# Mamba-2 stage: the convolutions of groups 2 to 5 begin one to three steps later, that of group 6 one step sooner

## Chip, cores and metric

One core of one Trainium2 chip runs the whole program. The metric is the time of one execution on the device in microseconds (us); of several executions the median is given. TensorE is written PE, VectorE DVE, ScalarE ACT, GpSimd POOL and SyncE SP, as in the profile.

## What is computed

A decoder trunk of two layers on 256 tokens of width 2048: attention with an MLP, then a Mamba-2 layer with an MLP, all in float32. The change lies in the Mamba-2 layer. Cut to what matters, it computes:

```python
zxbcdt = h @ w_in                                   # 2048 -> z 4096, x 4096, B 1024, C 1024, dt 64
xbc = silu(causal_depthwise_conv(xbc, conv_w, conv_b))     # 4 taps along the tokens
...
y_diag = einsum('blsgh,bsghp->blghp', cb[..., None] * decay, x_c)   # cb = C B^T per group, 8 groups of 8 heads
...
y = (y + d_skip * xs) * silu(z)
y = y * rsqrt(mean(y * y) + eps) * norm_g           # per group of 512 channels
return y @ w_out
```

The x channels fall into eight groups of 512. Each group needs its own convolution, its own 8 heads, its own gate with z and its own slice of the output projection.

## The kernel before

**Weights and PE.** All matmuls on weights are float32 made of three products: each weight tile is split into a rounded part `wh` (ACT, line 102) and the remainder `wl` (DVE, line 103). The unit of this work is a *half*: a tile of 128x1024 elements that holds 256 rows of a 512-wide weight block. The order listings number the halves: `wh557`, `wl557`. For each half `block` (line 328) issues 12 matmuls of 128x512 on PE: eight with `wh` (lines 339 and 340), then four with `wl` (line 343). Loads of raw halves run six ahead on SP's queue and conversions three ahead (`Flow`, line 72); there are four `wh` and four `wl` buffers, so a half can be converted once the half four places before it has been multiplied.

**Steps.** A block of 2048 rows has eight halves. After every two halves `block` calls `tick` (line 243). One such step runs whatever small pieces of work are due and then `pump` (line 1410), which handles up to two heads of the group in progress. A piece of work is placed by `self.later(n, fn)`: n steps after now. PE's order is the order in which the code issues. The instructions of DVE, ACT, POOL and SP are placed by the program's scheduler, so a piece need not stand exactly where its step was issued.

**The list.** In the second part of the Mamba-2 layer the order of blocks is the table `SSM_ORDER`: `B1` and `C1` are blocks of 8 halves for B and C, `z0` to `z7` the gate blocks, `o0a` to `o3` blocks of the output projection. A word `vg+n` is the convolution of group g. It has no matmul block of its own; it calls `x_conv(g, n)`, which places the pieces n steps after the block before it in the list:

```python
self.later(wait, lambda: fetch(whole, lambda: weight(3), lambda: load(2), lambda: weight(2), lambda: load(1)))
self.later(wait + 1, lambda: fetch(lambda: weight(1), lambda: load(0)))
self.later(wait + 3, mult)
self.later(wait + 4, some)
self.later(wait + 4, lambda: cb_group(g))
self.later(wait + 5, lambda: (total(), hq.extend((g, i) for i in range(8))))
self.later(wait + 6, tanh)
self.later(wait + 7, lambda: (silu(), ahead()))
```

**What one convolution issues.** On SP: the group's 128x1024 `xtm` tile and three shifted copies `tap` (512 KB each), and five weight rows `cw` (256 KB each). On DVE: line 1364 and three of line 1359 (tap times weight), four of line 1356 (adding them up), line 1384 (the end of silu), all of 128x1024; two of line 1311 (`cb`, 128x128) and line 1397 (`far`). On ACT: tanh (line 1380) and a part of `cb` (line 1316). On POOL: `ahead`'s product (line 1391). On PE: `cb` (lines 1307 and 1308), later `far` (line 1395). With `total` the group's heads enter the queue `hq`: per head four small ACT operations (lines 1431 and 1433), per four heads two DVE products (line 1438, `mt`). After the eighth head come `products` on PE (line 1451, 64 small matmuls), POOL's products (lines 1455 and 1457), `add` on DVE (line 1463), and two steps later `gate`: POOL (line 1491), ACT squares, DVE line 282, POOL's power (line 283), DVE lines 1495 and 1497, a DMA on POOL's queue (line 308), and three or four steps later transposes on PE, read out by lines 299 and 300. DVE also serves the z blocks (line 1479) and the output blocks (line 437).

Of the kernel before, what the change touches and what calls it, by code (L numbers as in the profile page):

```python
# [161 lines left out]
def part(key, src):  # L162

    def units(flow):
        ld = Load("raw", src)
        return [Unit(key, 2, 512, [ld], lambda: flow.halves(ld.tile, 1024))]
    return units
# [47 lines left out]
class Trunk:  # L215
# [959 lines left out]
    def ssm_body(self, sp, dp, gain, later):  # L1175
# [359 lines left out]

        for step in SSM_ORDER:
            kind, i = step[0], int(step[1])
# [11 lines left out]
            else:  # L1549
# [16 lines left out]
               [("x", 6, o) for o in range(3, 8)] + [("x", 7, o) for o in range(8)]]  # L1566
SSM_WEAVE = ("x x 0 x x 1 x x N40 2 x N41 x 3 x N42 M20 M21 x M22 M23 N43 x N30 N31 N32 N33",
             "x x 0 x x 1 x x N40 2 x x N41 3 x N42 M20 x M21 M22 x M23 N43 x N30 N31 N32 N33 x")
SSM_ORDER = ["v1+3", "B1", "C1", "v2+1", "z0", "z1", "v3", "z2", "z3", "v4", "o0a", "o0b", "v5", "z4", "z5", "v6", "o1a", "v7+1",
             "o1b", "z6", "z7", "o2a", "o2b", "o3"]  # L1570


def woven(p):
# [85 lines left out]
def sequence(d):  # L1659
# [45 lines left out]
    for p in range(2):  # L1705
        unit = seven(("s",), p, d["si"][:, 8:16])
        for tok in woven(p):
            if tok[0] == "s":
                seq.append(lambda flow, t=tok, unit=unit: [unit(flow, *t[2:])])
            else:  # L1710
                kind, i, o = tok
                seq.append(part(("si",) + tok, d["si"][o // 2, col(kind, i)][:, (o % 2) * 1024:(o % 2) * 1024 + 1024]))
    for step in SSM_ORDER:
        kind, i = step[0], int(step[1])
# [93 lines left out]
```

## Time and profile before

| | us |
|---|---|
| Median of 3 executions (2289.05 to 2290.42) | 2289.38 |
| The profiled execution, a separate one | 2292.69 |
| its span in the profile | 2290.9 |
| its PE busy | 2273.1 |
| its DVE busy | 1964.4 |
| its ACT busy | 1442.6 |
| its POOL busy | 284.9 |

The profile is of one execution; times in its views count from the start of the span. A row of a timeline gives start, duration, engine, line, operation, the tile written and the tiles read, how many instructions were merged, and in square brackets how long the engine was idle before it and what released it. The granted PE clock of this execution was 0.999 of full speed. The second part of the Mamba-2 layer, which `SSM_ORDER` sets, lies between about 1170 and 1610 us.

### The profile page before, as it was taken

Reading aid. Unit: us, or ns where it says so; the run is one execution under the profiler, and the core shown is the slowest. Engines: PE = TensorE matmul, PEld = TensorE weight load, DVE = VectorE, ACT = ScalarE, POOL = GpSimd, SP = SyncE. Lnnn points to the kernel's source line nnn. Section 1 sums busy time; section 2 is a strip of 40 time slices with the busy share of each in tenths; the row PEclk is TensorE's granted clock in tenths of the full one; section 3 lists DMA queues with packets and bytes.
Section 4 is the critical chain, followed back from the end, with each engine's and each line's share of the span. In section 5 each row is a group of like instructions: output and inputs, shape, how many; then the busy total and the mean of one; then the engine's idle time right before and its main releaser. Section 6 shows DMA issues by size and latency. Waiting matters only on the chain.

```text
span 2290.9 us, 30854 instructions
## 1 busy us (share of the span) xinstructions
PE 2273.1 (99%) x10881; PEld 1881.4 (82%) x10881; DVE 1964.4 (86%) x2257; ACT 1442.6 (63%) x2044; POOL 284.9 (12%) x339
## 2 busy tenths in 40 slices
PE   9999999999999999999999999999999999999999
PEld 7898888888888888887788788888888887888887
DVE  7786698999899897888889998976989988989985
ACT  7775476566566666566577676564666665666663
POOL 1440000000000000100002532230000000000000
PEclk9999999999999999999999999999999999999999
DMA  8545678888888877758798888866788887798874
GB/s 315 172 152 163 210 234 264 261 253 263 269 253 261 268 231 246 244 180 281 234 359 288 290 289 303 307 215 218 211 261 252 256 275 234 253 277 243 266 232 163
DMA packets 176026, 569.74 MB, mean 249 GB/s; under 512 B 20192, under 2 KB 29344, under 8 KB 175872
## 3 DMA queue, kind: packets, MB, share of 16 engines
q1 hardware_dynamic: 147808, 498.24, 64.9%
q0 software_dynamic: 16320, 56.88, 11.8%
q10 hardware_dynamic: 11744, 12.66, 1.7%
q8 instruction: 85, 1.39, 0.2%
q14 instruction: 69, 0.57, 0.1%
HBM read 542.23 MB, written 6.41 MB: 239 GB/s over the span
## 4 chain that ended last, share of the span: by engine, by line
PE 87%; DVE 6%; DMA 4%; issue 2%; ACT 1%; POOL 0%; SPq 0%; ACTq 0%; DVEq 0%
PE acc L339 10%; PE acc L340 10%; PE acc L343 10%; PE yp L618 9%; PE yp L619 8%; PE yp L617 8%; PE st L618 7%; PE st L619 7%; PE st L617 7%; DVE wl L103 3%; DMA wraw<-mi 2%; DMA wraw<-si 1%; ACT wh L102 1%; PE st L1162 1%; PE st L1160 1%
## 5 line engine op out<-in xcount | busy, mean ns | idle before, releaser
L102 ACT ACTIVATE wh<-wraw 128x1024 fp32r<-128x1024 f32 (+1 forms) x818 | 857.5, 1053 | 528.5 <-PE acc L340 176.7
L103 DVE TENSOR_TENSOR wl<-wraw,wh 128x1024 fp32r<-128x1024 f32 (+1 forms) x818 | 989.2, 1227 | 180.5 <-ACT wh L102 169.7
L617 PE MATMUL yp<-wh,k 128*128 128x512 f32 x896 | 349.7, 390 | 0.0
L618 PE MATMUL yp<-wl,k 128*128 128x512 f32 x896 | 349.1, 390 | 0.1
L619 PE MATMUL yp<-wh,k 128*128 128x512 f32 x896 | 349.0, 390 | 0.0
L102 ACT ACTIVATE wh<-wrx 128x1024 fp32r<-128x1024 f32 x192 | 203.2, 1059 | 174.8 <-PE yp L619 98.4
L103 DVE TENSOR_TENSOR wl<-wrx,wh 128x1024 fp32r<-128x1024 f32 x192 | 233.0, 1219 | 37.1 <-ACT wh L102 36.2
L618 PEld LDWEIGHTS yp<-wl,k 128*128 128x128 f32 x896 | 168.5, 188 | 35.5 <-DVE wl L103 0.5
L619 PEld LDWEIGHTS yp<-wh,k 128*128 128x128 f32 x896 | 168.5, 188 | 35.2
L339 PE MATMUL acc<-wh,k 128*128 128x512 f32 x496 | 196.9, 397 | 0.3 <-ACT k L299 0.3
L617 PEld LDWEIGHTS yp<-wh,k 128*128 128x128 f32 x896 | 168.5, 188 | 34.9
L340 PE MATMUL acc<-wh,k 128*128 128x512 f32 x496 | 193.7, 391 | 0.6 <-DVE k L300 0.6
L339 PE MATMUL acc<-wh,xt 128*128 128x512 f32 x480 | 191.8, 400 | 0.6 <-ACT wh L102 0.6
L340 PE MATMUL acc<-wh,xt 128*128 128x512 f32 x480 | 187.7, 391 | 0.0
L617 PE MATMUL st<-wh,xt 128*128 128x512 f32 x448 | 177.7, 397 | 0.0
L619 PE MATMUL st<-wh,xt 128*128 128x512 f32 x448 | 174.9, 390 | 0.0
L618 PE MATMUL st<-wl,xt 128*128 128x512 f32 x448 | 174.7, 390 | 0.0
L199 POOL DMA_DIRECT2D wrx<-mi x56 | 49.1, 877 | 726.1 <-DVE wl L103 515.5
L617 PE MATMUL st<-wh,sN 128*128 128x512 f32 x336 | 133.4, 397 | 0.8 <-ACT wh L102 0.8
L618 PE MATMUL st<-wl,sN 128*128 128x512 f32 x336 | 131.8, 392 | 2.1 <-DVE wl L103 2.0
L343 PE MATMUL acc<-wl,k 128*128 128x512 f32 x496 | 132.7, 389 | 0.0
L619 PE MATMUL st<-wh,sN 128*128 128x512 f32 x336 | 131.4, 391 | 0.0
(342 smaller groups left out, 3806.6 us busy)
## 6 DMA issues: line engine op xcount, KB each, us to landing
wraw<-mi SPq DMA_DIRECT2D x256, 512.0 KB, 5.7
wraw<-mo SPq DMA_DIRECT2D x256, 512.0 KB, 5.2
wraw<-si SPq DMA_DIRECT2D x160, 512.0 KB, 5.7
wraw<-so SPq DMA_DIRECT2D x64, 512.0 KB, 5.1
wrx<-mi SPq DMA_DIRECT2D x56, 512.0 KB, 5.2
wrx<-mi POOLq DMA_DIRECT2D x56, 512.0 KB, 7.7
wraw<-wo SPq DMA_DIRECT2D x32, 512.0 KB, 4.1
tap<-xD SPq DMA_DIRECT2D x24, 512.0 KB, 8.3
```

Source lines behind the costliest of these rows:

```text
L102: self.last = nc.scalar.activation(h[:, v], raw[:, v], AF.Copy)
L103: self.last_lo = nc.vector.tensor_tensor(lo[:, v], raw[:, v], h[:, v].bitcast(F32), ALU.subtract)
L199: nc.gpsimd.dma_start(st["b11"].tile, quarter(d, 1, 0), accum_op=ALU.add)
L339: nc.tensor.matmul(accs[t][:, :n], ah, wh[:, q, :], start=first and kt + q == 0, stop=False)
L340: nc.tensor.matmul(accs[t][:, :n], al, wh[:, q, :], start=False, stop=False)
L343: nc.tensor.matmul(accs[t][:, :n], lhs(kt + q, t)[0], wl[:, q, :], start=False, stop=en and q == nk - 1)
L617: nc.tensor.matmul(b, ah, wh, start=first and q == 0, stop=False)
L618: nc.tensor.matmul(b, ah, wl, start=False, stop=False)
L619: nc.tensor.matmul(b, al, wh, start=False, stop=last and q == 1)
L1160: nc.tensor.matmul(bank[onto], ah, wh, start=done + q == 0 and not skip, stop=False, skip_group_check=skip)
L1162: nc.tensor.matmul(bank[onto], ah, wl, start=False, stop=done == 3 and q == 1, skip_group_check=skip)
```

## The change

One table is written anew; no function changes.

```diff
-SSM_ORDER = ["v1+3", "B1", "C1", "v2+1", "z0", "z1", "v3", "z2", "z3", "v4", "o0a", "o0b", "v5", "z4", "z5", "v6", "o1a", "v7+1",
-             "o1b", "z6", "z7", "o2a", "o2b", "o3"]
+SSM_ORDER = ["v1+3", "B1", "C1", "v2+2", "z0", "z1", "v3+1", "z2", "z3", "v4+3", "o0a", "o0b", "v5+1", "z4", "v6+3", "z5", "o1a",
+             "v7+1", "o1b", "z6", "z7", "o2a", "o2b", "o3"]
```

Convolutions 2, 3 and 5 begin one step later and 4 three steps later. Convolution 6 stood behind `z5` and now stands behind `z4` with three steps to wait; a z block has four steps, so it begins one step sooner. From one convolution's start to the next's there were 6, 7, 8, 8, 8, 5 steps (1 to 2, 2 to 3, and so on to 7), and there are now 7, 7, 10, 6, 6, 6. The sequence of weight halves is the same, and so are the counts of rows on PE (10011), SP (999) and POOL (336); ACT and DVE differ only in how like rows are merged.

DVE between the halves 554 and 556, in blocks `z0` and `z1`. Before:

```order
L103 TENSOR_TENSOR wl554_11473<-wraw554_11372,wh554_11472 128x1024
L1230 SCALAR_TENSOR_TENSOR s2_824_11413<-s2_825_11414,cst_96,s2_824_11413 128x253
L1364 TENSOR_TENSOR xtm2_11300<-xtm2_11300,cw2_3_11302 128x1024
L1359 TENSOR_TENSOR tap2_2_11304<-tap2_2_11304,cw2_2_11306 128x1024
L1233 SCALAR_TENSOR_TENSOR k4_813_11155<-s2_826_11424,s2_824_11413 128x512
L1479 SCALAR_TENSOR_TENSOR s2_828_11442<-s2_828_11442,acc_816_11160 128x512
L1479 SCALAR_TENSOR_TENSOR s2_829_11445<-s2_829_11445,acc_817_11161 128x512
L1356 TENSOR_TENSOR xtm2_11300<-xtm2_11300,tap2_2_11304 128x1024
L103 TENSOR_TENSOR wl555_11527<-wraw555_11390,wh555_11526 128x1024
L282 TENSOR_SCALAR st_837_11503<-st_827_11441 128x2
L103 TENSOR_TENSOR wl556_11545<-wraw556_11452,wh556_11544 128x1024
```

and now:

```order
L103 TENSOR_TENSOR wl554_11473<-wraw554_11368,wh554_11472 128x1024
L1230 SCALAR_TENSOR_TENSOR s2_824_11409<-s2_825_11410,cst_96,s2_824_11409 128x253
L1438 TENSOR_TENSOR mt12_11508<-mt12_11508,cb1_11133 128x512 x2
L103 TENSOR_TENSOR wl555_11520<-wraw555_11386,wh555_11519 128x1024
L1233 SCALAR_TENSOR_TENSOR k4_813_11155<-s2_826_11420,s2_824_11409 128x512
L1479 SCALAR_TENSOR_TENSOR s2_828_11442<-s2_828_11442,acc_816_11160 128x512
L1479 SCALAR_TENSOR_TENSOR s2_829_11445<-s2_829_11445,acc_817_11161 128x512
L103 TENSOR_TENSOR wl556_11538<-wraw556_11452,wh556_11537 128x1024
```

The three pieces of group 2's convolution (`xtm2`, `tap2_2`) have left, and the score products of group 1 (`mt12`) have moved up.

DVE between the halves 556 and 557, just behind. Before:

```order
L103 TENSOR_TENSOR wl556_11545<-wraw556_11452,wh556_11544 128x1024
L1495 TENSOR_TENSOR st_839_11507<-st_838_11504,rs0_150 128x2
L1359 TENSOR_TENSOR tap2_1_11308<-tap2_1_11308,cw2_1_11353 128x1024
L1497 SCALAR_TENSOR_TENSOR s2_828_11442<-xtm0_10549,st_839_11507,gb_834_11495 128x512
L1497 SCALAR_TENSOR_TENSOR s2_829_11445<-xtm0_10549,st_839_11507,gb_834_11495 128x512
L1356 TENSOR_TENSOR xtm2_11300<-xtm2_11300,tap2_1_11308 128x1024
L1311 SCALAR_TENSOR_TENSOR cb2_11565<-sm_842_11562,tri_8827 128x128 x2
L1397 TENSOR_TENSOR far1_11570<-sm_843_11568,edge_8831 128x512
L1438 TENSOR_TENSOR mt12_11515<-mt12_11515,cb1_11133 128x512 x2
L103 TENSOR_TENSOR wl557_11587<-wraw557_11470,wh557_11586 128x1024
```

and now:

```order
L103 TENSOR_TENSOR wl556_11538<-wraw556_11452,wh556_11537 128x1024
L1364 TENSOR_TENSOR xtm2_11343<-xtm2_11343,cw2_3_11345 128x1024
L282 TENSOR_SCALAR st_837_11496<-st_827_11441 128x2
L1359 TENSOR_TENSOR tap2_2_11347<-tap2_2_11347,cw2_2_11349 128x1024
L1495 TENSOR_TENSOR st_839_11500<-st_838_11497,rs0_150 128x2
L1397 TENSOR_TENSOR far1_11562<-sm_842_11560,edge_8831 128x512
L1497 SCALAR_TENSOR_TENSOR s2_828_11442<-xtm0_10549,st_839_11500,gb_834_11488 128x512
L1497 SCALAR_TENSOR_TENSOR s2_829_11445<-xtm0_10549,st_839_11500,gb_834_11488 128x512
L1356 TENSOR_TENSOR xtm2_11343<-xtm2_11343,tap2_2_11347 128x1024
L103 TENSOR_TENSOR wl557_11579<-wraw557_11470,wh557_11578 128x1024
```

Between `wl554` and `wl557` there stood five 128x1024 pieces of group 2 and its two `cb` pieces; three 128x1024 pieces stand there now, and the other two and the `cb` pieces follow behind `wl558`.

DVE between the halves 616 and 617, in block `o1b`, where the convolution of group 6 runs. Before:

```order
L103 TENSOR_TENSOR wl616_13393<-wraw616_13320,wh616_13392 128x1024
L1364 TENSOR_TENSOR xtm6_13243<-xtm6_13243,cw6_3_13245 128x1024
L1359 TENSOR_TENSOR tap6_2_13247<-tap6_2_13247,cw6_2_13249 128x1024
L437 TENSOR_TENSOR x01_143<-acc_941_13318,x01_143 128x512
L1356 TENSOR_TENSOR xtm6_13243<-xtm6_13243,tap6_2_13247 128x1024
L437 TENSOR_TENSOR x11_147<-acc_942_13319,x11_147 128x512
L103 TENSOR_TENSOR wl617_13422<-wraw617_13338,wh617_13421 128x1024
```

and now:

```order
L103 TENSOR_TENSOR wl616_13364<-wraw616_13291,wh616_13363 128x1024
L1359 TENSOR_TENSOR tap6_1_13125<-tap6_1_13125,cw6_1_13218 128x1024
L1311 SCALAR_TENSOR_TENSOR cb6_13384<-sm_935_13381,tri_8827 128x128
L1356 TENSOR_TENSOR xtm6_13117<-xtm6_13117,tap6_1_13125 128x1024
L1311 SCALAR_TENSOR_TENSOR cb6_13384<-sm_935_13381,tri_8827 128x128
L1397 TENSOR_TENSOR far5_13389<-sm_936_13387,edge_8831 128x512
L1497 SCALAR_TENSOR_TENSOR s2_915_12902<-xtm4_12422,st_942_13403,gb_937_13391 128x512
L1438 TENSOR_TENSOR mt44_13334<-mt44_13334,cb5_13002 128x512 x2
L437 TENSOR_TENSOR x01_143<-acc_933_13289,x01_143 128x512
L437 TENSOR_TENSOR x11_147<-acc_934_13290,x11_147 128x512
L103 TENSOR_TENSOR wl617_13430<-wraw617_13309,wh617_13429 128x1024
```

The second tap of group 6, its `cb`, the `far` part and the score products of group 5 and a gate product of group 4 now stand together in front of one half.

## The prediction

> **What bounds the kernel now.** First the page: its head, the busy times and the chain of work that ended last.
>
> ```profile
> span 2290.9 us, 30854 instructions
> ...
> PE 2273.1 (99%) x10881; PEld 1881.4 (82%) x10881; DVE 1964.4 (86%) x2257; ACT 1442.6 (63%) x2044; POOL 284.9 (12%) x339
> ...
> PE 87%; DVE 6%; DMA 4%; issue 2%; ACT 1%; POOL 0%; SPq 0%; ACTq 0%; DVEq 0%
> ```
>
> PE is busy for 2273.1 of 2290.9 us, so all its pauses together are 17.8 us. The change adds no PE instruction and removes none. It can only win or lose PE's pauses, and only those in the stretch it touches. Those are shown by PE's waits between 1170 and 1580 us (total, times, longest):
>
> ```profile
> engine line waited for: us in total, times, longest us
> PE acc L343 <- DVE wl L103: 2.6, 1, 2.6
> PE acc L340 <- DVE k L300: 0.6, 1, 0.6
> PE acc L339 <- ACT k L299: 0.3, 1, 0.3
> ```
>
> There are three, 3.5 us together, and one of them is 2.6 us. The timeline of PE shows where it stands:
>
> ```profile
> 1262.75 1.07 PE L343 MATMUL acc<-wl,xt 128*128 128x512 f32 x4
> ...
> 1265.25 0.39 PE L340 MATMUL acc<-wh,xt 128*128 128x512 f32 x1
> 1268.22 1.19 PE L343 MATMUL acc<-wl,xt 128*128 128x512 f32 x4 [2.58 <-DVE wl L103]
> 1269.34 2.09 PE L1451 MATMUL y<-xtm,mt 128*64 128x64 f32 x64
> ```
>
> The last `wh` matmul of a half starts at 1265.25, and the four `wl` matmuls come only at 1268.22, after 2.58 us of idling. The 64 small matmuls of group 1 behind them name the half: it is 557, the last of `z0`'s. Why its `wl` was late is in DVE's timeline.
>
> ```profile
> 1250.63 0.48 DVE L1230 SCALAR_TENSOR_TENSOR s<-s,cst,s 128x253 f32<-128x253 f32 x1
> 1251.02 1.22 DVE L1364 TENSOR_TENSOR xtm<-xtm,cw 128x1024 f32<-128x1024 f32 x1
> 1252.16 1.22 DVE L1359 TENSOR_TENSOR tap<-tap,cw 128x1024 f32<-128x1024 f32 x1
> 1253.29 0.69 DVE L1233 SCALAR_TENSOR_TENSOR k<-s,s 128x512 f32<-128x512 f32 x1
> 1253.89 1.28 DVE L1479 SCALAR_TENSOR_TENSOR s<-s,acc 128x512 f32<-128x512 f32 x2
> 1255.09 1.92 DVE L1356 TENSOR_TENSOR xtm<-xtm,tap 128x1024 f32<-128x1024 f32 x1
> 1256.93 2.31 DVE L103 TENSOR_TENSOR wl<-wraw,wh 128x1024 fp32r<-128x1024 f32 x1
> 1259.17 0.15 DVE L282 TENSOR_SCALAR st<-st 128x2 f32<-128x2 f32 x1
> 1259.24 1.21 DVE L103 TENSOR_TENSOR wl<-wraw,wh 128x1024 fp32r<-128x1024 f32 x1
> 1261.06 0.16 DVE L1495 TENSOR_TENSOR st<-st,rs 128x2 f32<-128x2 f32 x1 [0.62 <-POOL st L283]
> 1261.14 1.23 DVE L1359 TENSOR_TENSOR tap<-tap,cw 128x1024 f32<-128x1024 f32 x1
> 1262.29 1.41 DVE L1497 SCALAR_TENSOR_TENSOR s<-xtm,st,gb 128x512 f32<-128x512 f32 x2
> 1263.61 1.22 DVE L1356 TENSOR_TENSOR xtm<-xtm,tap 128x1024 f32<-128x1024 f32 x1
> 1264.75 0.48 DVE L1311 SCALAR_TENSOR_TENSOR cb<-sm,tri 128x128 f32<-128x128 f32 x2
> 1265.15 0.68 DVE L1397 TENSOR_TENSOR far<-sm,edge 128x512 f32<-128x512 f32 x1
> 1265.74 1.28 DVE L1438 TENSOR_TENSOR mt<-mt,cb 128x512 f32<-128x512 f32 x2
> 1266.94 2.35 DVE L103 TENSOR_TENSOR wl<-wraw,wh 128x1024 fp32r<-128x1024 f32 x2
> ```
>
> The last row holds `wl557` and `wl558`; the first of them ends near 1268.1. No bracket stands at that row, so the copy `wh557` was there and DVE simply came late. Between 1250.6 and 1268.1 it paused once, for 0.62 us. This is a queue on a full engine.
>
> **The change, part by part.** *The late half.* By the two orders, DVE's work between `wl554` and `wl557` loses one L1359, one L1356 and two L1311 (front, first two places). From start to start these took 1.15 (1261.14 to 1262.29), 1.14 (1263.61 to 1264.75) and 0.40 (1264.75 to 1265.15): 2.69 us. The score products of group 1 move up but are counted in both. So `wl557` ends near 1268.1 - 2.7 = 1265.4, and PE wants it 2.58 before 1268.22, at 1265.64. The wait goes, with 0.2 us to spare. A second gain stands beside it: an L1359 now lies between L282 and L1495 and covers the 0.62 us pause for POOL's power. I take the gain at 2.6 us. Its bounds are 1.7 (one more row slowed as at 1256.93, 2.31 us instead of 1.22, less the 0.2 to spare) and 2.6, for a wait cannot give more than itself.
>
> *What is late next.* With PE 2.6 us earlier every later half is wanted 2.6 us earlier, while DVE, which has no free time there, does the same work: by wl561 both orders have done the same. The next thin place is half 565, here its `wl` on DVE and its matmuls on PE:
>
> ```profile
> 1287.30 2.32 DVE L103 TENSOR_TENSOR wl<-wraw,wh 128x1024 fp32r<-128x1024 f32 x1
> ...
> 1293.13 1.07 PE L343 MATMUL acc<-wl,xt 128*128 128x512 f32 x4
> ```
>
> It was ready 1293.13 - 1289.62 = 3.5 us ahead. After the change that is 3.5 - 2.6 = 0.9, plus 0.6 for one L1438 that now stands behind it: 1.5 us. That holds, so I cost it at nothing; one slowed row (1.1 us) fits, two do not.
>
> *Groups 4 to 6, six steps apart instead of eight.* The convolution work taken out of the earlier part lands here. Adding the orders' rows from `wl589` to `wl637` (1.14 us per 128x1024 row, 0.60 per 128x512, and 0.40, 0.20 and 0.67 for L1230, L1311 and L1497, all start to start as above), DVE has 117.9 us of work before and 129.8 after. The window between those two halves shows how full it was (us, DVE busy):
>
> ```profile
> 1363.80:1501.00 137.20, 127.16 (x139) 1.00 0.85 294
> ```
>
> 127.2 busy of 137.2. So 117.9 of table work cost 9.3 us more than the table, and 10.0 us were free; 11.9 more nearly fill it. What decides is the lead, how long a half is ready before PE wants it. Where DVE waits for buffers alone the lead is full:
>
> ```profile
> 1386.78 1.22 DVE L103 TENSOR_TENSOR wl<-wraw,wh 128x1024 fp32r<-128x1024 f32 x1 [1.24 <-ACT wh L102]
> ...
> 1395.85 1.07 PE L343 MATMUL acc<-wl,xt 128*128 128x512 f32 x4
> ```
>
> That is half 599: 1395.85 - 1388.00 = 7.8 us. PE's own pace is in three more of its rows, the matmuls with `wl` of halves 566, 567 and 568:
>
> ```profile
> 1296.75 1.07 PE L343 MATMUL acc<-wl,xt 128*128 128x512 f32 x4
> 1299.47 1.07 PE L343 MATMUL acc<-wl,xt 128*128 128x512 f32 x4
> 1302.87 1.07 PE L343 MATMUL acc<-wl,xt 128*128 128x512 f32 x4
> ```
>
> A half alone takes 2.72 us (1296.75 to 1299.47), `cb`'s matmuls behind half 567 add 0.68 (3.40 to the next), `far`'s behind 565 add 0.90 (1293.13 to 1296.75 is 3.62). In the new order DVE's rows outrun PE at three places. Between halves 588 and 593 it has 16.6 us against 14.3 (five halves and a `cb`), between 613 and 617 15.2 against 12.5 (four, `cb`, `far`; the third place in the front), between 624 and 629 18.7 against 15.2 (five, `cb`, `far`). The lead falls by 2.3, 2.7 and 3.5, to 5.5, 5.1 and 4.3. The extra 9.3 us are four groups' to the window, 2.3 each, and leave 3.2, 2.8 and 2.0. So these three cost nothing either; from below nothing is to be won, since PE did not wait here, and from above the bound is the slower rival below.
>
> *What else moves, at nothing.* SP's loads of a convolution move with it, ahead of other weight loads than before; ACT's longest wait for weights shows what that can do:
>
> ```profile
> ACT wh L102 <- DMA wraw<-si: 14.1, 10, 3.3
> ```
>
> 3.3 us at most, ten times, and none reached PE; a full lead of 7.8 covers it. If the lead is down to 4.3 it still does. ACT (63% busy) and POOL keep their instructions. PE's small blocks stand behind other halves; each takes its time wherever it stands, and I allow 0.3 us either way for neighbours. The waits of 0.6 and 0.3 us are those of group 7's transposes, which keep their place.
>
> *The sum.* 2292.69 - 2.6 = 2290.1 for an execution like the profiled one (span 2288.3). The profiled one was 3.3 us above the median of 2289.38, so the median goes to 2289.38 - 2.6 + 0.1 = **2286.9**. A measurement of this kernel can tell about 0.2%, 4.6 us, from no change; the forecast is a gain of 0.11%.
>
> **What POOL does to this sum.** Two of its rows and one where DVE stood still:
>
> ```profile
> 1254.65 3.51 POOL L1491 TENSOR_TENSOR xtm<-s,xtm 128x512 f32<-128x512 f32 x2 [12.08 <-DVE s L1479]
> ...
> 1271.46 10.41 POOL L1455 TENSOR_TENSOR xtm<-xtm,gb 128x512 f32<-128x512 f32 x2 [6.13 <-issue]
> ...
> 1501.87 2.54 POOL L1455 TENSOR_TENSOR xtm<-xtm,gb 128x512 f32<-128x512 f32 x2 [3.08 <-issue]
> ```
>
> A pair of POOL products takes 2.54 us alone and 10.41 beside a DVE that never pauses; and DVE rows beside L1491 took 1.92 and 2.31 instead of 1.22. Either may pay. The Trainium skill, SBUF — State Buffer, "Who interferes with whom", says that a VectorE instruction with two SBUF inputs contends with a GpSimd one that reads SBUF, and that whoever issues first keeps the shared ports for its whole instruction while the other stands. By that rule, with POOL always first, DVE is charged the whole of each POOL instruction and the sum is the slower rival's 2296.5; with DVE always first it is the forecast's. The rows above agree that one side stands, and here it is mostly POOL.
>
> **Rivals.** *The wait moves* (0.20). PE, no longer held at 557, is held at 565 or at one of the three crowded places, because two rows are slowed there. For it: 565's lead is only 1.5 us. Against it: everywhere else 2 us and more are left. Price: two slowed rows, 2.2 us, or one with the 0.8 us that L1495 can wait (L282 and L1495 now stand together ahead of `wl566`), against 1.5: about 0.7 each time, twice 1.3. Time 2288.2.
>
> *Nothing happens* (0.07). The late half stays late: the loss of 2.7 us of rows is made up by other slow rows, as POOL's L1491 falls on L1364 and `wl556` now. Against it: L1491 starts when L1479 ends, and the rows ahead of L1479 last as long in both orders (two of 1.14 before, one of 1.14 and two of 0.60 now). Time 2289.4.
>
> *Slower* (0.09). Between halves 588 and 629 DVE is nearly full, and it pays for POOL. Six POOL products per group at 1.27 us are 7.6, with the pause of 0.6 before L1495 8.2 us per group. Against leads of 5.5, 5.1 and 4.3 this makes waits of 2.7, 3.1 and 3.9, 9.7 in all; less 2.6 the kernel is 7.1 us slower, 2296.5. It turns against the change from about 5.8 us per group on, where the three waits sum to 2.5. Against it stands the 2.3 per group measured in that window.
>
> **How the numbers follow.** The forecast has 0.64. Its own range is 2285.9 (the other two waits shrink as well) to 2288.0. The range 2285.9 to 2289.6 takes in the forecast, the moved wait and the unchanged case; the slower rival is left out. For over 0.2% faster 4.6 us would be needed, and this stretch has 3.5 us of waits: 0.02. For over 0.2% slower, half of the slower rival: 0.05. Within 0.2%: 0.93.
>
> **What would show it.** Right: no PE wait for `wl` at half 557 between 1170 and 1580 us; DVE ending `wl557` before L340 of that half is done; the same 2.0 us of small matmuls behind it; DVE's busy share between halves 589 and 637 near 139 of 138 us of PE time, that is with hardly a pause, and no PE wait there; about 1.5 us of lead at 565. Wrong: a wait of PE for `wl` at 565, 593, 617 or 629; DVE rows of over 2 us in numbers; PE's spacing of 2.72 us per half changed.

## The result, and the profile after

The changed kernel takes 2298.73 us (median of 6 runs, 2294.64 to 2303.03) against 2289.9 us for the one before (6 runs, 2288.6 to 2292.85): 1.0039 times as long, interval 1.0029 to 1.0049. That is 8.8 us or 0.39% slower, where 0.11% faster was forecast; it lies outside the range given. The profiled execution took 2298.48 us.

The page of the kernel after: its head, the busy times and the chain that ended last.

```profile
span 2296.7 us, 30847 instructions
...
PE 2277.0 (99%) x10881; PEld 1882.1 (82%) x10881; DVE 1970.8 (86%) x2257; ACT 1442.1 (63%) x2044; POOL 280.0 (12%) x339
...
PE 91%; DVE 3%; DMA 3%; ACT 1%; issue 1%; POOL 1%; SPq 0%; DVEq 0%; ACTq 0%; POOLq 0%
```

PE has the same 10881 instructions, but is busy for 3.9 us longer (2273.1 before). So besides the pauses something made its instructions themselves slower. PE's waits of the kernel after, between 1170 and 1580 us (total, times, longest):

```profile
PE sm L1395 <- DVE k L300: 4.6, 1, 4.6
PE acc L339 <- ACT k L299: 1.3, 1, 1.3
PE acc L343 <- DVE wl L103: 1.1, 1, 1.1
PE acc L340 <- DVE k L300: 0.3, 1, 0.3
```

There were three waits of 3.5 us in all; there are four of 7.3. Where they stand is in PE's timeline of the kernel after. The first and last rows are marks: the transposes behind half 549, the products behind 557, and the products behind half 641, between which PE has the same work in both kernels.

```profile
1243.31 0.60 PE L1220 MATMUL sm<-ident,s 128*128 128x128 f32 x4
...
1267.62 2.09 PE L1451 MATMUL y<-xtm,mt 128*64 128x64 f32 x64
...
1281.42 1.21 PE L343 MATMUL acc<-wl,xt 128*128 128x512 f32 x4 [1.10 <-DVE wl L103]
...
1327.32 0.50 PE L339 MATMUL acc<-wh,k 128*128 128x512 f32 x1 [1.27 <-ACT k L299]
1328.13 0.50 PE L340 MATMUL acc<-wh,k 128*128 128x512 f32 x1 [0.30 <-DVE k L300]
...
1405.12 0.59 PE L1307 MATMUL sm<-k,k 128*128 128x256 f32 x2
...
1405.69 0.53 PE L322 MATMUL sm<-ident,tr 128*128 128x128 f32 x4
1410.84 1.63 PE L1395 MATMUL sm<-s,cb 128*128 128x512 f32 x2 [4.62 <-DVE k L300]
1411.48 1.41 PE L339 MATMUL acc<-wh,xt 128*128 128x512 f32 x1
1412.69 0.63 PE L340 MATMUL acc<-wh,xt 128*128 128x512 f32 x1
1413.12 0.63 PE L339 MATMUL acc<-wh,xt 128*128 128x512 f32 x1
...
1534.97 2.08 PE L1451 MATMUL y<-xtm,mt 128*64 128x64 f32 x64
```

The same marks in the kernel before (that of 557 stands in the prediction, at 1269.34):

```profile
1242.63 0.60 PE L1220 MATMUL sm<-ident,s 128*128 128x128 f32 x4
...
1524.66 2.09 PE L1451 MATMUL y<-xtm,mt 128*64 128x64 f32 x64
```

From 549 to 557 PE took 26.71 us before and 24.31 after: 2.40 us are won, nearly what was forecast, and of the wait at 557 a stop of 0.12 us is left. From 557 to 641 it took 255.32 before and 267.35 after: 12.03 us are lost, so between these marks the kernel is 9.6 us slower. The medians differ by 8.8 us and the two profiled executions as a whole by 5.8 (spans 2290.9 and 2296.7): behind half 641 the one before took 4.5 us more, 1.7 of it by a stretch of halved clock at 1908.55. In the 12.03 are

- 1.10 us at half 561, the wait for `wl`;
- 1.57 us at half 576, the first that multiplies group 1's transposed gate output (lines 299 and 300);
- 4.62 us behind half 601, where `far` of group 4 (line 1395) waits;
- slow matmuls behind the last two. At 1412.69 and 1413.12 they follow each other in 0.43 us and not in 0.23.

The windows of the kernel after, behind those two waits (us, busy PE, PEld, DVE, ACT, POOL, then the granted PE clock):

```profile
1329.60:1333.00 3.40, 3.40 (x10) 2.64 (x9) 3.40 (x5) 3.24 (x9) 0.72 (x1) 0.54 0.46 153
1411.40:1414.80 3.40, 3.40 (x9) 2.34 (x8) 1.12 (x2) 0.00 (x0) 0.00 (x0) 0.52 0.69 194
```

For 3.41 us each the clock is halved, and half of that time is lost: 1.7 us each, 3.4 together. With the waits, 7.29 by their brackets, that makes 10.7. The other 1.3 us lie mostly at the same places and in a stop of 0.12 us at 1294.0, since a wait costs more than its bracket: at half 561 the last `wh` row starts at 1279.93 and the `wl` row at 1281.42, 1.49 us apart where 0.23 is usual, which is 1.26 us for a bracket of 1.10.

Why `far` waited is in DVE's timeline of the kernel after:

```profile
1407.22 1.22 DVE L1359 TENSOR_TENSOR tap<-tap,cw 128x1024 f32<-128x1024 f32 x1
1408.47 1.22 DVE L1356 TENSOR_TENSOR xtm<-xtm,tap 128x1024 f32<-128x1024 f32 x1
1409.62 0.48 DVE L1311 SCALAR_TENSOR_TENSOR cb<-sm,tri 128x128 f32<-128x128 f32 x2
1410.02 0.68 DVE L300 TENSOR_TENSOR k<-sm,k 128x512 fp32r<-128x512 f32 x1
1410.61 1.21 DVE L103 TENSOR_TENSOR wl<-wraw,wh 128x1024 fp32r<-128x1024 f32 x1
```

`far`, `cb` and these transposes all write into the pool `sm`, which has two banks (line 229: `self.sm = pool("sm", 2, space=PSUM)`). A bank here is a tile in PSUM, the memory that PE writes its results to; the program gives it to the next block only when the readers of the last one are done. Behind half 601 the new order issues three of them in one step: `cb` of group 5, a transpose of group 3, `far` of group 4. The bank of `cb` is kept until ACT has read it, one step later (`far_part`). `far` needs the other one, and that holds the transposes, which PE had written by 1406.2. DVE reads them in line 300 behind two long rows of convolution 5 and the `cb` rows, from 1410.02 to 1410.70; at 1410.84 PE goes on. In the order before, `far` of group 4 stood behind half 611 with nothing else of `sm` there, and it did not wait:

```profile
1432.99 1.02 PE L1395 MATMUL sm<-s,cb 128*128 128x512 f32 x2
```

### The profile page after: what moved, and what is told of

Read it like the earlier page. It is cut to its first block, busy times and chain, and to the rows that moved or that the text cites. A ratio compares the mean times of both kernels' runs of the same rounds, so it can differ in the third digit from the quotient of the medians.

```text
span 2296.7 us, 30847 instructions
## 1 busy us (share of the span) xinstructions
PE 2277.0 (99%) x10881; PEld 1882.1 (82%) x10881; DVE 1970.8 (86%) x2257; ACT 1442.1 (63%) x2044; POOL 280.0 (12%) x339
## 4 chain that ended last, share of the span: by engine, by line
PE 91%; DVE 3%; DMA 3%; ACT 1%; issue 1%; POOL 1%; SPq 0%; DVEq 0%; ACTq 0%; POOLq 0%
PE acc L339 10%; PE acc L340 10%; PE acc L343 9%; PE yp L619 9%; PE yp L617 9%; PE yp L618 9%; PE st L618 7%; PE st L619 7%; PE st L617 7%; DVE wl L103 2%; DMA wraw<-si 1%; PE st L1162 1%; PE yp L339 1%; PE yp L340 1%; PE sm L324 1%
```

## The experiments

All kernels are changed from the one after. The order tables are given by the words that differ. "Stretch" is the time from PE's products behind 557 to those behind 641, as above: 255.32 us before, 267.35 after. The kernel before was timed again beside each group of runs, with medians of 2289.82 to 2290.40 us; distances from it are from the median beside the run. Each experiment was profiled in one execution.

**A bank of another pool for one block**

```diff
-                    b = self.bank(False)
+                    b = self.yp.tile([P, 512], F32, tag="yp", name=self.name("yp")) if g == 4 else self.bank(False)
```

> The changed order; only the far product of group 4 (line 1395) is written to a bank of the pool yp instead of sm. Bank theory (behind half 601 three blocks, cb of group 5, group 3's transposes and far of group 4, want three banks of a pool of two, so far waits for the read of the transposes, 4.62 us, and the half-rate clock stretch behind that pause costs 1.7 us more): no wait of PE at line 1395, no half-rate stretch near 1411 us, and 4 to 6.5 us less than the changed kernel: about 2293 us, 1.5 to 4 us above the kernel before. Rival (DVE is full there, and whatever it reads out late stops PE): the wait of 3 us and more turns up within the next four halves, at a wl matmul or at the transposes of half 603, and the time stays within 1.5 us of the changed kernel's 2298.7.

Measured: 2291.44 us (2289.41 to 2294.24), 1.0005 times the kernel before (0.9997 to 1.0014): 7.3 us below the changed kernel, a little more than was expected. PE's timeline, and DVE's, of this kernel:

```profile
1404.79 0.54 PE L322 MATMUL sm<-ident,tr 128*128 128x128 f32 x4
1405.16 1.09 PE L1395 MATMUL yp<-s,cb 128*128 128x512 f32 x2
1405.69 0.79 PE L339 MATMUL acc<-wh,xt 128*128 128x512 f32 x1
```

```profile
1410.41 0.68 DVE L300 TENSOR_TENSOR k<-sm,k 128x512 fp32r<-128x512 f32 x1
```

DVE reads the transposes 5.1 us after PE has written them (3.8 in the changed kernel), but `far` runs straight on at 1405.16 and nothing waits for that. No PE wait follows until 1575, so the wait did not move on. The window behind it shows the full clock:

```profile
1411.40:1414.80 3.40, 3.40 (x19) 2.81 (x18) 3.40 (x4) 1.96 (x3) 0.00 (x0) 1.00 0.44 105
```

The bank theory holds; the rival, a DVE so full that it stops PE in any case, falls. The stretch is 259.52 us, 7.8 less than in the changed kernel. The bank's share of that is 6.3, the wait of 4.62 and the 1.7 of halved clock behind it. Most of the rest is luck of this execution: no halved clock followed the wait at 576 (1.24 and 0.30 us).

**Only the early part of the change**

```diff
-"v4+3", "o0a", "o0b", "v5+1", "z4", "v6+3", "z5"
+"v4", "o0a", "o0b", "v5", "z4", "z5", "v6"
```

> Only convolutions 2 and 3 begin one step later, groups 4 to 6 stand as before. By the bank theory there is no half with three blocks, so no wait at line 1395; the gain of 2.4 us at half 557 is given back at 561 (1.1 to 1.3 us, wl) and at 576 (1.6 us, the tiles of group 1's transposes, with a half-rate stretch of 1.7 us behind it): 0 to 3 us above the kernel before, and 6 to 9 us below the changed kernel. Rival (the early part alone makes DVE late for good): 5 us and more above the kernel before.

Measured: 2292.4 us (2287.75 to 2297.96), 1.0009 (1.0 to 1.0018), 2.3 us above the kernel before. No wait at line 1395; at 576 PE waits 1.17 and 0.31 us. The profiled execution, 2287.75, was the shortest of the twelve, and it has no wait at 561. DVE and POOL of this execution there, then of the changed kernel:

```profile
1267.65 2.35 DVE L103 TENSOR_TENSOR wl<-wraw,wh 128x1024 fp32r<-128x1024 f32 x2
...
1268.30 7.38 POOL L1455 TENSOR_TENSOR xtm<-xtm,gb 128x512 f32<-128x512 f32 x2 [5.01 <-issue]
```

```profile
1270.16 4.36 DVE L103 TENSOR_TENSOR wl<-wraw,wh 128x1024 fp32r<-128x1024 f32 x2
...
1269.75 3.69 POOL L1455 TENSOR_TENSOR xtm<-xtm,gb 128x512 f32<-128x512 f32 x2 [3.94 <-issue]
```

The rows are the same, `wl559` and `wl560` on DVE and group 1's products on POOL. Where POOL starts before the `wl` pair, its products take 3.69 us and DVE's pair 4.36; where it starts behind, 7.38 and 2.35. So the wait at 561 goes with which of the two starts first, and that differs between executions with the same early order.

**Only the late part**

```diff
-"v2+2", "z0", "z1", "v3+1"
+"v2+1", "z0", "z1", "v3"
```

> Only convolutions 4 to 6 are moved; groups 2 and 3 stand as before. Here too half 601 has cb of group 5, transposes and far of group 4 behind it. Bank theory: PE's wait of 2.6 us at 557 is back, none at 561 or 576, and at line 1395 behind 601 a wait of 3 to 6 us with a half-rate stretch behind it: 4 to 8 us above the kernel before. Rival (the crowding of groups 4 to 6 costs only because PE came early by the first part): no wait at 1395 over 1 us, within 1.5 us of the kernel before.

Measured: 2296.81 us (2296.08 to 2302.11), 1.0033 (1.0021 to 1.0045), 6.7 us above the kernel before. PE's waits, and the window behind the first of them:

```profile
PE sm L1395 <- DVE k L300: 5.0, 1, 5.0
PE acc L343 <- DVE wl L103: 3.1, 1, 3.1
```

```profile
1408.80:1415.50 6.70, 5.14 (x10) 3.49 (x11) 2.11 (x5) 0.00 (x0) 0.00 (x0) 0.50 0.66 209
```

The wait comes without the early part, and two half-rate stretches in a row follow it in this execution, the slowest of the five. The two halves of the change cost 2.3 and 6.7 us alone, 9.0 together, against 8.8 for both.

**One step less for group 4**

```diff
-"v4+3"
+"v4+2"
```

> The changed order with v4+2 in place of v4+3: convolution 4 one step sooner, so far of group 4 stands behind half 599, and behind 601 only cb of group 5 and transposes, two banks. Bank theory: no wait at line 1395, waits at 561 and 576 as in the changed kernel (1.1 and 1.6 us): 4 to 6.5 us below the changed kernel, about 2293 us. Rival (DVE full between 588 and 629 stops PE in any case): a wait of 3 us and more in that stretch and a time within 1.5 us of the changed kernel's.

Measured: 2292.97 us (2290.24 to 2298.1), 1.0015 (1.0007 to 1.0024), 5.8 us below the changed kernel. The size is as the bank theory says, but in part by luck: in this execution a wait was left that it had not foreseen, and the wait at 561, which it expected, was absent (POOL's pair took 7.74 us).

```profile
PE sm L322 <- DVE far L1397: 2.4, 1, 2.4
```

`far` now stands behind half 599. Its bank is wanted again behind 601, for the transposes, while `cb` of group 5 holds the other, and DVE had not yet read `far` out (line 1397). Counting the blocks of one step is too lenient; a block of the step before counts as long as its reader has not run. At half 593 PE waits 0.44 us for `wl`.

**POOL's products of group 1 left out, on the kernel of the first experiment**

```diff
-                for t in range(2):
+                for t in range(2 * (g != 1)):
                     x = xg[g][t]
                     nc.gpsimd.tensor_tensor(x, x, dg, ALU.mult)
```

> The kernel of e1_far4_bank without POOL's three products of group 1 (lines 1455 and 1457): the term d_skip * xs and the far part of y are left out for that group. Theory (DVE's slow rows between wl558 and the L1359 behind wl560, 2.18 and 2.32 us instead of 1.2, are POOL's doing, and they are why PE waits at 561): those rows take 1.2 us each, 3 us less together, PE has no wait at 561 (1.10 us in e1), and the time is 1 to 2 us below e1's 2291.4. Rival (DVE is full there with or without POOL): the wait at 561 stays at 0.8 us or more and the time is within 0.7 us of e1.

Measured: 2289.4 us (2286.49 to 2291.83), 0.9999 (0.999 to 1.0008). The time is 2 us below the first experiment's, less than the two intervals can tell apart. The trace has no wait at 561, and the DVE pair is

```profile
1269.66 2.35 DVE L103 TENSOR_TENSOR wl<-wraw,wh 128x1024 fp32r<-128x1024 f32 x2
```

as long as where POOL comes second; the row of line 1356 behind it takes 1.22 us (2.32 in the first experiment). Over the profiled executions of the early part with POOL's products in, 561 has a wait of 1.10 or 1.11 us in the four where POOL's pair took 3.68 or 3.69 us, and none in the four where it took 7.38 to 7.82. In the first four PE had also stopped at 557 (0.12 to 1.38 us), in the other four not, so DVE's lateness at 557 alone could have been the cause. This run speaks against that: PE stops at 557 for 0.74 us and still does not wait at 561. It has another wait for a bank, 0.71 us at the transposes behind half 603 (line 322).

**Convolution 3 where it was, on the kernel of the first experiment**

```diff
-"v3+1"
+"v3"
```

> The kernel of e1_far4_bank with v3 in place of v3+1. Theory (PE waits 1.5 us at half 576 because ACT's read-out of group 1's transposes, line 299, is queued behind the tanh of convolution 3, line 1380, which waits 5.2 us for DVE): with convolution 3 a step sooner the tanh is through before them, no wait of PE at lines 339 and 340 near 1328 us; 1 to 2 us below e1, about 2290. Rival (the transposes are late for another reason, DVE's read of its half, line 300): the wait at 576 stays at 1 us or more.

Measured: 2291.76 us (2289.51 to 2294.98), 1.001 (1.0001 to 1.0019): no less than the first experiment. ACT before half 576, in the changed kernel and then in this one:

```profile
1323.62 1.06 ACT L1380 ACTIVATE th<-xtm 128x1024 f32<-128x1024 f32 x1 [5.19 <-DVE xtm L1356]
...
1326.69 1.07 ACT L299 ACTIVATE k<-sm 128x512 fp32r<-128x512 f32 x2
```

```profile
1314.95 1.06 ACT L1380 ACTIVATE th<-xtm 128x1024 f32<-128x1024 f32 x1 [5.84 <-DVE xtm L1356]
...
1323.34 0.57 ACT L299 ACTIVATE k<-sm 128x512 fp32r<-128x512 f32 x1
```

With the tanh a step earlier, ACT's reads start 3.35 us sooner, and PE's wait at line 339 is gone. Of the 1.5 us there 0.51 is left, at line 340, for DVE's read. The mechanism was right. But the time did not follow: `wl` waits of 0.32 and 0.40 us stand at 1303 and 1309 in its place; ahead of the first, lines 1364, 1359 and 1356 of convolution 3 stand in DVE's queue now, ahead of the second lines 1359, 1311 and 1356. The stretch is 257.74 us against 259.52 in the first experiment, but 1.1 us of that is the wait at 561, which this execution does not have (POOL's pair took 7.82 us).

**Only one word of the change**

```diff
-"v2+2", "z0", "z1", "v3+1", "z2", "z3", "v4+3", "o0a", "o0b", "v5+1", "z4", "v6+3", "z5"
+"v2+2", "z0", "z1", "v3", "z2", "z3", "v4", "o0a", "o0b", "v5", "z4", "z5", "v6"
```

> The order of before with v2+2 as the only word changed. Theory: the wait at 557 falls from 2.6 to 0 to 1.2 us, 561 may cost up to 1.1 us, no wait at 576 (convolution 3 where it was), no wait at line 1395: 0 to 2.5 us below the kernel before, about 2289. Rival (what is taken from 557 comes back later whatever stands behind it): a new wait of 1.5 us and more between 561 and 600, time at or above the kernel before.

Measured: 2291.19 us (2286.56 to 2296.61), 1.0006 (0.9997 to 1.0016). Not the gain that was expected. PE's timeline has

```profile
1267.77 1.20 PE L343 MATMUL acc<-wl,xt 128*128 128x512 f32 x4 [1.38 <-DVE wl L103]
...
1282.68 1.20 PE L343 MATMUL acc<-wl,xt 128*128 128x512 f32 x4 [1.11 <-DVE wl L103]
```

that is a wait at 557 after all and one at 561 (POOL first, 3.69 us), then 0.32, 0.40 and 0.54 us as in the run above. Its stretch is 259.84 us. No single wait of 1.5 us came back, so the rival is not borne out as stated, but what 557 gives is spent in small pieces before half 577.

**Filling the pause with work: four products, then seven**

```diff
                 def across():
+                    if g == 4:
+                        spare = self.yp.tile([P, 512], F32, tag="yp", name=self.name("yp"))
+                        for _ in range(4):
+                            nc.tensor.matmul(spare, cb[g][:, P:256], xw, start=True, stop=True)
```

> The changed kernel; between the transposes behind half 601 and far of group 4 PE computes four more products of the shape of far into a spare bank, which nothing reads (about 0.9 us each, 3.6 of the 4.6 us that it waits). Clock theory (the half-rate stretch of 3.41 us behind 1411 us comes from the pause): no half-rate stretch there, the five matmuls behind far are spaced 0.23 us and not 0.43; the wait itself stays, as about 1 us behind the four products; 1 to 2 us below the changed kernel, about 2297. Rival (the stretch comes from something else, as the load at that time): it stays, and the time with it.

Measured: 2298.22 us (2295.29 to 2300.72), 1.0036 (1.0022 to 1.005). The half-rate stretch stayed, but this does not speak for the rival, since the pause stayed too. PE and its clock in the window behind:

```profile
1402.09 3.67 PE L1397 MATMUL yp<-s,cb 128*128 128x512 f32 x8
1409.22 1.12 PE L1399 MATMUL sm<-s,cb 128*128 128x512 f32 x2 [3.46 <-DVE k L300]
```

```profile
1410.50:1414.00 3.50, 3.50 (x10) 2.70 (x9) 0.57 (x1) 0.61 (x1) 0.00 (x0) 0.52 0.74 191
```

(Line 1399 is `far` here.) In this execution PE had no wait at 561 and no half-rate stretch behind 576, and came 4 us sooner than in the changed kernel (1401.71 for the transposes), DVE with its line 300 only 1.5 us; so PE stood at this bank for 3.67 + 3.46 = 7.1 us and not 4.62. So 2.5 us of the 4.0 that were gained ahead of this place were lost at it. The run told nothing about the clock, so it was made again with seven (`range(7)`):

> As e8_fill with seven products in the place of four (0.92 us each there, so 6.4 us against a wait that was 4.62 us in the changed kernel and 3.67 + 3.46 = 7.1 us in e8). Clock theory (a pause of some 3 us is what brings a half-rate stretch): the pause left at far is under 1.5 us, no half-rate stretch follows it, and PE's wh matmuls behind it are spaced 0.23 us; 0 to 2 us below the changed kernel, since the products take time of their own where they last longer than the wait. Rival (the stretch has nothing to do with the pause): it stands there as in e8, with 0.43 us spacing.

Measured: 2295.97 us (2293.75 to 2297.56), 1.0023 (1.0013 to 1.0032). PE and two windows of it:

```profile
1406.02 6.24 PE L1397 MATMUL yp<-s,cb 128*128 128x512 f32 x14
1412.10 1.02 PE L1399 MATMUL sm<-s,cb 128*128 128x512 f32 x2
```

```profile
1329.60:1333.00 3.40, 3.40 (x11) 2.63 (x10) 3.40 (x5) 3.22 (x9) 0.75 (x1) 0.62 0.46 151
...
1412.60:1416.00 3.40, 3.40 (x16) 2.63 (x15) 0.69 (x1) 1.01 (x2) 0.00 (x0) 1.00 0.84 245
```

With no pause at 1410 the granted clock behind it is 1.00, and PE gets through 16 instructions in 3.40 us where the changed kernel had 9. The pause of 1.57 us at 576, which was left as it was, still brings its stretch at 1329. So the half rate comes from the pauses. The median is 2.8 us below the changed kernel's, but the two intervals overlap. In the traces the stretch is 266.89 us against 267.35: what the whole clock gave, 1.7 us, the products took nearly all again, 6.24 us in place of a wait of 4.62.

**Only the late part, with the other bank**

The order of the third experiment and the edit of the first.

> The order of e3_late (only groups 4 to 6 moved) with far of group 4 in a bank of yp as in e1. Theory (the crowding of DVE by groups 4 to 6 costs PE nothing; all that e3 lost, 6.7 us, was the wait of far for a bank and the clock behind it): PE's wait of 2.6 to 3.1 us at 557 stays, none of over 0.7 us between 588 and 650, time within 1.5 us of the kernel before. Rival (the crowding costs by itself): 2 us and more above the kernel before, with waits for wl at 593, 617 or 629.

Measured: 2291.96 us (2287.9 to 2295.53), 1.0005 (0.9996 to 1.0014); the medians differ by 1.56 us, a hair over what was expected, and the interval holds no difference. PE's wait at 557 was 1.37 us, less than the 2.6 to 3.1 expected. The window that the prediction read in the kernel before, here:

```profile
1363.80:1501.00 137.20, 137.20 (x777) 112.83 (x777) 130.15 (x142) 88.61 (x168) 48.93 (x34) 1.00 0.84 293
```

DVE does 130.2 us of work instead of 127.2 in this window and PE does not stop at all. From `wl589` to `wl637` DVE works for 139.3 of 146.9 us, against 127.1 of 137.1 before, 12.2 more. The stretch is 255.42 us, against 255.32 before. By the trace the crowding of groups 4 to 6 on DVE costs nothing, and the loss of the late part was one bank; by the medians 5.1 of its 6.7 us are gone, and the interval allows all.

No version was below the kernel before by more than its interval. Not tried: a version that sets which of POOL and DVE starts first at `wl559`.

## Why the prediction was wrong, step by step

- **The bound, and the late half: right.** PE's pauses decide, and the wait at 557 shrank. From 549 to 557 PE took 26.71, 28.36 and 25.50 us in the three profiled executions with the old early order (28.36 holds 0.9 us lost to a halved clock), 26.9 in the mean, and 23.90 to 25.57 in the nine with the new one, 24.6 in the mean. That is 2.3 us, 0.3 of it that one halved clock; 2.6 was forecast. The wait at 557 itself differs between executions of the old early order, 2.58, 3.15 and 1.37 us, and the prediction had one of them. The 0.2 us to spare were too few to be sure of: 557 still waited 0.7 to 1.4 us in four of the nine.
- **"What is late next": wrong in the place.** It named half 565, with 1.5 us of lead; there the lead was 1.8 us and held. The next waits were at 561 (1.10 us) and 576 (1.57). The step took POOL's cost as paid by POOL, as in the execution before (10.41 us for its pair); with DVE's rows moved, POOL started first in half of the executions and DVE paid, 2 us in `wl559` and `wl560` alone. The rule of the Trainium skill weighed there (SBUF — State Buffer, "Who interferes with whom": who issues first keeps the ports) agrees with the traces, 3.69 us for POOL's pair and 4.36 for DVE's with POOL first, 7.38 and 2.35 with DVE first; the error was to take one order of the two as given. And half 576 was not looked at, because only `wl` was followed: a half of an output block needs its transposed gate output too, and that read stands in ACT's queue behind the tanh of convolution 3.
- **Groups 4 to 6 on DVE: right.** No wait at 593, 617 or 629 in the changed kernel, and none in the tenth experiment. There the leads (end of the `wl` row to PE's row of line 343) were 3.2, 2.4 and 2.1 us, where 3.2, 2.8 and 2.0 were forecast, and DVE's work grew by 12.2 us, where 11.9 was forecast. In the first experiment, with both parts of the change and the other bank, they were 2.3, 0.2 and 0.05: next to nothing was left.
- **"PE's small blocks stand behind other halves; each takes its time wherever it stands, and I allow 0.3 us either way": this step failed.** They take their time, but they also take a bank each, of two, until DVE and ACT have read it. The order listing of PE would have shown `cb`, transposes and `far` behind one half, and line 229 the two banks. In place of the 0.3 us it cost 4.6 us of waiting and 1.7 of halved clock behind it, 6.3 in the trace; the first experiment, without that wait, is 7.3 us below the changed kernel by the medians.
- **The clock: a term that was missing.** Every pause was priced at its own length. Two of them cost 1.7 us more each.
- **The slower rival had the sign and nearly the size (2296.5) for another reason.** Its mechanism, DVE paying for POOL between 588 and 629, brought no wait, so that its number came near is luck.

## What to carry to other kernels

When small blocks of work move against each other, count for each step which of them write to the same pool of PSUM banks, and how long each bank is held: up to the reader's place in its engine's queue, not up to the end of the write. A gain ahead of the next such place is worth little, since PE waits there longer: 2.5 of 4.0 us were lost so in the run with four products. A pause of PE of about 1.5 us or more can cost 1.7 us beyond its length: seven of the twelve here did.

## What the runs showed of the hardware

- **The clock behind a pause.** PE's granted clock falls to 0.50 for 3.413 us, by the clock's record in the trace, and once for twice that. In the part that the change touches, pauses of 5.04, 4.62, 3.46, 3.15 and 2.38 us brought it. Of six pauses of about 1.5 us at 576 (two waits 0.8 us apart) two did and four did not, and that of 2.58 us in the kernel before did not. The Trainium skill (TensorE: Matmul & The Clock Gate, "What's actually happening") describes a free-running window of 3413 ns, and half the clock after an idle one. The length agrees. That 1.57 us of idling, under half a window, can be enough, and that 2.58 us need not be, does not fit a rule that wants a whole idle window.
- **Where a pause falls decides in the main.** The traces show it when their time is cut into windows of 3.413 us. In the changed kernel the three half-rate stretches begin at 1104.07, 1329.35 and 1411.27, which is 66 and 24 times 3.413 us apart, so the grid can be laid over the whole trace (in traces without such a stretch, by the one at their end). The pauses at 576 that brought a stretch lay in one window (1.58 and 1.57 us idle in it); those that did not were split, 1.17 to 1.27 us in one window and 0.3 in the next. The 2.58 us of the kernel before were split into 1.21 and 1.37, and the 5.04 us, with two stretches behind it, into 3.33 and 1.72. Over the twelve traces, from 20 to 2285 us, each window with 1.96 us of idling or more was followed by the half rate, none with 1.54 or less was, and between them both occur. A few matmul records can be missing, so these bounds are rough. The window ahead of the stretch at 1329.35 in the changed kernel, and the two that share the pause of 2.58 us in the one before (us, busy PE first):

```profile
1325.94:1329.35 3.41, 1.83 (x7) 1.02 (x7) 3.10 (x5) 3.41 (x7) 0.00 (x0) 1.00 0.64 189
```

```profile
1263.39:1266.81 3.42, 2.24 (x10) 1.51 (x9) 3.42 (x7) 1.55 (x3) 1.67 (x3) 1.00 0.71 229
1266.81:1270.22 3.41, 2.00 (x34) 1.55 (x36) 3.41 (x4) 2.59 (x4) 0.00 (x0) 1.00 0.40 108
```

- **Who pays, DVE or POOL, is settled within less than a microsecond.** The same two pairs of instructions cost DVE 4.36 us and POOL 3.69, or DVE 2.35 and POOL 7.38. In the four executions of the first kind POOL started 0.40 to 0.43 us ahead of DVE's pair, in the four of the second 0.20 to 0.65 behind it. POOL starts when PE has done the products behind half 557 (0.04 us behind them in the changed kernel). In the first four PE had stopped at 557, in the others not. This and the clock may be why executions of one kernel differ by up to 10.2 us (2287.75 to 2297.96 in the second experiment); no kernel was profiled twice, so that is not shown.
